# A two-layer decoder trunk: the 14 additions that close Strassen's scheme in each FFN, asked for in three portions

## The chip, the cores and the metric

The kernel runs on one core of one Trainium2 chip. The metric is the time of one execution in device microseconds (us). A profiled execution has a span, from its first to its last instruction, and a time of its own that is a little longer.

## The reference

A sequence of 512 tokens with 1024 features goes through two layers: a retention layer with its FFN, then a dilated-attention layer with its FFN. All is float32. Only the FFNs matter here, and both have this form:

```python
def conv_ffn(h, w_up, conv_w, conv_b, w_down):
    S = h.shape[1]
    u = h @ w_up                                   # 1024 -> 2 * 2816
    gate, val = u[..., :D_FF], u[..., D_FF:]
    gp = jnp.pad(gate, ((0, 0), (CONV_WIDTH - 1, 0), (0, 0)))
    conv = conv_b
    for i in range(CONV_WIDTH):
        conv = conv + conv_w[i] * gp[:, i:i + S]
    return (jax.nn.gelu(conv, approximate=True) * val) @ w_down   # 2816 -> 1024
...
x = x + rmsnorm(f, norm_ffn_post[layer])
```

## The kernel before, in words

**Products in three matmuls.** Every float32 operand is split into a high part (a cast to fp32r) and a low part (what the cast lost). A product is then high x high, high x low and low x high: `mm3`, lines 210 to 212. For a weight unit of 128x1024 this means one load into a `raw` tile (line 157, on SP's queue, three buffers), one cast on ScalarE into `whi` (line 170) and one subtraction on VectorE into `wlo` (line 171); `whi` and `wlo` have five buffers each, so a cast waits until TensorE has finished with the unit five places earlier.

**The FFN.** The 2816 inner features are 22 rows of 128 features, f = 0 to 21. `up(f)` loads two units of w_up (gate and value), forms two products of 24 matmuls each (8 steps of 3) into two PSUM tiles `pm`, and `gated` turns them into an activation (convolution at lines 599 to 604, gelu at 605, product at 607, split at 612). In this document "f=19 gate" is the unit, or the product, of the gate half of row 19.

**Strassen's scheme.** The rows 2 to 17 go through w_down in four groups of four rows. A group (`down7`, `contract7`) forms seven products instead of eight, in the order 1, 7, 6, 4, 5, 2, 3, each for two blocks of rows r = 0, 1: 12 matmuls of the `po` kind per number, 84 per group. Each result is added from PSUM into a running sum in SBUF (line 273). The sums lie in the tiles that are free for that time: product 1 in the first halves of m0 and m1, product 3 in their second halves, product 4 and 5 in the halves of m2 and m3, and products 2, 6 and 7 in tiles called q0, q1 and q2, which take the places of the residual tiles x0, x1 and x2. For that, x was written out to DRAM before (`away`, line 696). PSUM has two buffers for the sums of r = 0 and four, shared with `pm`, for those of r = 1.

**The end of the scheme.** The last group is formed behind `up(18)`. `combine7` (line 327) then joins the seven sums: for each r it adds 6+=1, 1+=2, 5+=6, 3+=5, 5+=7, 4+=6, 4+=7, so 14 additions of 128x512 on VectorE (line 332). Behind it, in the text of the program, x0 to x3 are loaded back (line 710; x3 shared its place with no sum, so its load comes much earlier), then come `up(19)` to `up(21)`, then `contract` over the rows 0 and 1, and then `finish`, which contracts over the rows 18 to 21, normalises, and adds to x (line 351).

**What sets the order.** Each engine runs its instructions in a fixed order, and each queue its transfers. The program is compiled by a scheduler that takes the text's order as priority and a model of the times to decide when an instruction is placed on its engine; in the stretches that matter here it is free on all engines (`finish` fixes the order of VectorE and GpSimd by hand). What an engine waits for at run time is set by data and by buffers.

Of the kernel before, what the change touches and what calls it, by code (L numbers as in the profile page):

```python
# [10 lines left out]
F32 = mybir.dt.float32  # L11
# [6 lines left out]
P = 128  # L18
SEQ = 512
D = 1024  # L20
NB = SEQ // P
# [54 lines left out]
def _run(gen):  # L76
    for _ in gen:
        pass
# [18 lines left out]
def trunk(ctx: ExitStack, tc: tile.TileContext, a, out):  # L97
    nc = tc.nc

    const = ctx.enter_context(tc.tile_pool(name="const", bufs=1))  # L100
# [5 lines left out]
    away = [dram.tile([P, D], F32, name=f"away{b}") for b in range(NB)]  # L106
# [6 lines left out]
    x = [const.tile([P, D], F32, name=f"x{b}", tag=f"x{b}") for b in range(NB)]  # L113
# [94 lines left out]
    def mm3(o, l, r, start, stop):  # L208

        nc.tensor.matmul(o, lhsT=l[0], rhs=r[0], start=start, stop=False)  # L210
        nc.tensor.matmul(o, lhsT=l[0], rhs=r[1], start=False, stop=False)  # L211
        nc.tensor.matmul(o, lhsT=l[1], rhs=r[0], start=False, stop=stop)  # L212
# [56 lines left out]
    def accumulate(src, dst, first):  # L269
        if first:  # L270
            nc.scalar.copy(out=dst, in_=src)
        else:
            nc.vector.tensor_add(out=dst, in0=src, in1=dst)  # L273

    def contract(left, w, first, tag="po", after=None):


        for b in range(NB):
            for c in range(2):
                po = ps.tile([P, 512], F32, name="po", tag=tag, bufs=4 if tag == "mm" else 2)  # L280
                for j in range(len(w)):
                    mm3(po, left(j, b), (w[j][0][:, half(c)], w[j][1][:, half(c)]), j == 0, j == len(w) - 1)
                    if j < len(w) - 1:
                        yield
                accumulate(po, m[b][:, half(c)], first)
                if after is not None:
                    after(b, c)
                yield
# [38 lines left out]
    def combine7(q):  # L327

        for r in range(2):
            q1, q2, q3, q4, q5, q6, q7 = (q[i][r] for i in range(1, 8))  # L330
            for dst, src in ((q6, q1), (q1, q2), (q5, q6), (q3, q5), (q5, q7), (q4, q6), (q4, q7)):
                nc.vector.tensor_add(out=dst, in0=dst, in1=src)  # L332

    E = mybir.EngineType
    F4=1
# [251 lines left out]
    def ffn(l, pool, post, then, late, ahead=()):  # L587
        w_up, w_down = a["ffn_w_up"][l], a["ffn_w_down"][l]
        cw = lambda i, f: cols[l][:, i * FT + f : i * FT + f + 1]
        with pool as tmp:  # L590
# [30 lines left out]
            SEVEN = 2, 18  # L621
# [65 lines left out]
            def down(fs, act, pool=None):  # L687
                w = [unit(w_down[f * P : (f + 1) * P, :], pool=pool if i < 3 else None) for i, f in enumerate(fs)]
                return lambda j, b: [t[:, blk(b)] for t in act[j]], w
# [7 lines left out]
            q = {i: [m[r + 2 * h][:, half(c)] for r in range(2)] for i, h, c in ((1, 0, 0), (3, 0, 1), (4, 1, 0), (5, 1, 1))}  # L697
# [3 lines left out]
            for f in range(2, FT):  # L701
                acts[f] = up(f)
                f0 = f - 4
                if seven(f0) and f0 % 4 == 2:
                    down7(f0, [acts[f0 + i] for i in range(4)], group[f0], f0 == SEVEN[0], q)
                    if f == SEVEN[1]:
                        combine7(q)
                        for b in range(NB):
                            x[b] = const.tile([P, D], F32, name=f"x{b}", tag=f"x{b}")
                            nc.sync.dma_start(out=x[b], in_=away[b])  # L710
                if seven(f) and f % 4 == 1:
                    group[f - 3] = list(sx)
            _run(contract(*down(range(2), [acts[0], acts[1]]), False))
            prev = (range(FT - 4, FT), [acts[f] for f in range(FT - 4, FT)])
            l, w = down(*prev, tmp)
# [415 lines left out]
```

## Time and profile before

| what | value |
|---|---|
| time, median of 3 runs | 1720.17 us (1720.15 to 1720.6) |
| time of the profiled execution | 1719.35 us |
| its span | 1717.5 us |
| mean granted TensorE clock | 0.993 of full speed |
| TensorE busy | 1682.1 us (98%) |
| VectorE busy | 1083.7 us (63%) |
| ScalarE busy | 661.9 us (39%) |
| GpSimd busy | 389.8 us (23%) |

The first FFN lies at about 411 to 798 us of the span, the second from about 1340 us to the end. In a timeline row the first number is the start (us from the span's start), the second the length in us, then engine, line, operation and tiles, and in brackets how long the engine was idle before it and what ended that. PE is TensorE, DVE VectorE, ACT ScalarE, POOL GpSimd, SP the queue of the transfers. The matmuls overlap: their lengths are longer than the distance from one start to the next, and it is the distance that counts. Consecutive instructions of VectorE overlap a little at their ends too. Some matmul records are missing from a trace.

### The profile page before, as it was taken

Reading aid. Unit: us, or ns where it says so; the run is one execution under the profiler, and the core shown is the slowest. Engines: PE = TensorE matmul, PEld = TensorE weight load, DVE = VectorE, ACT = ScalarE, POOL = GpSimd, SP = SyncE. Lnnn points to the kernel's source line nnn. Section 1 sums busy time; section 2 is a strip of 40 time slices with the busy share of each in tenths; the row PEclk is TensorE's granted clock in tenths of the full one; section 3 lists DMA queues with packets and bytes.
Section 4 is the critical chain, followed back from the end, with each engine's and each line's share of the span. In section 5 each row is a group of like instructions: output and inputs, shape, how many; then the busy total and the mean of one; then the engine's idle time right before and its main releaser. Section 6 shows DMA issues by size and latency. Waiting matters only on the chain. (4 is left out here: it accounts for less than half of the span.)

```text
span 1717.5 us, 21852 instructions
## 1 busy us (share of the span) xinstructions
PE 1682.1 (98%) x8494; PEld 1394.2 (81%) x8494; DVE 1083.7 (63%) x1718; ACT 661.9 (39%) x1170; POOL 389.8 (23%) x281
## 2 busy tenths in 40 slices
PE   8999999999999999999899999999999999999998
PEld 6888888887888888788788888888887888888876
DVE  4553545558666787868556556566465866777875
ACT  5232322325454444343143243243254545434431
POOL 1000000004000000036756655665531400000003
PEclk9999999999999999999999999999999999999999
DMA  6422323214523422331322322222221533233041
GB/s 208 129 71 86 88 90 92 75 60 157 163 74 99 135 84 77 123 120 51 96 74 74 87 74 67 82 75 78 83 74 58 186 100 111 74 110 123 25 147 49
DMA packets 208565, 164.52 MB, mean 96 GB/s; under 512 B 5245, under 2 KB 182349, under 8 KB 208462
## 3 DMA queue, kind: packets, MB, share of 16 engines
q1 hardware_dynamic: 208462, 163.12, 30.7%
q8 instruction: 67, 1.10, 0.3%
q14 instruction: 36, 0.29, 0.1%
HBM read 156.81 MB, written 6.29 MB: 95 GB/s over the span
## 5 line engine op out<-in xcount | busy, mean ns | idle before, releaser
L171 DVE TENSOR_TENSOR wlo<-raw,whi 128x1024 fp32r<-128x1024 f32 x299 | 405.1, 1359 | 223.7 <-ACT whi L170 222.3
L212 PE MATMUL pm<-hT_hi,wlo 128*128 128x512 f32 (+1 forms) x1424 | 539.3, 379 | 6.8 <-DVE wlo L171 6.8
L210 PE MATMUL pm<-hT_hi,whi 128*128 128x512 f32 (+1 forms) x1424 | 545.8, 383 | 0.0
L211 PE MATMUL pm<-hT_lo,whi 128*128 128x512 f32 (+1 forms) x1424 | 538.9, 378 | 0.0
L170 ACT CAST whi<-raw 128x1024 fp32r<-128x1024 f32 x299 | 313.0, 1051 | 530.7 <-PE pm L211 255.4
L212 PEld LDWEIGHTS pm<-hT_hi,wlo 128*128 128x128 f32 x1424 | 268.6, 189 | 58.1 <-DVE wlo L171 7.7
L210 PEld LDWEIGHTS pm<-hT_hi,whi 128*128 128x128 f32 x1424 | 269.0, 189 | 51.2 <-issue 3.2
L211 PEld LDWEIGHTS pm<-hT_lo,whi 128*128 128x128 f32 x1424 | 269.0, 189 | 48.1 <-DVE hT_lo L201 0.9
L160 POOL TENSOR_TENSOR raw<-raw,cols 128x1024 f32<-128x1024 f32 x72 | 139.7, 1941 | 448.1 <-DMA raw<-in_att_w_kv 374.1
L210 PE MATMUL pm<-whi,hT_hi 128*128 128x512 f32 (+1 forms) x384 | 141.9, 369 | 0.0
L211 PE MATMUL pm<-wlo,hT_hi 128*128 128x512 f32 (+1 forms) x384 | 136.7, 356 | 0.0
L212 PE MATMUL pm<-whi,hT_lo 128*128 128x512 f32 (+1 forms) x384 | 136.7, 356 | 0.0
L369 POOL TENSOR_TENSOR h<-m,gain 128x512 f32<-128x512 f32 x28 | 42.0, 1498 | 397.9 <-issue 329.1
L273 DVE TENSOR_TENSOR m<-po,m 128x512 f32<-128x512 f32 x112 | 75.3, 685 | 45.3 <-PE po L212 45.0
L217 POOL TENSOR_TENSOR r_gn<-v_gn,nhalf 128x1 f32<-128x1 f32 x16 | 8.8, 550 | 357.4 <-DVE v_gn L526 357.4
L211 PE MATMUL po<-wlo,ah 128*128 128x512 f32 x224 | 87.8, 392 | 0.0
L210 PE MATMUL po<-whi,ah 128*128 128x512 f32 x224 | 87.8, 392 | 0.0
L212 PE MATMUL po<-whi,al 128*128 128x512 f32 x224 | 87.6, 391 | 0.0
L210 PEld LDWEIGHTS pm<-whi,hT_hi 128*128 128x128 f32 x384 | 72.9, 190 | 11.5 <-issue 1.0
L211 PEld LDWEIGHTS pm<-wlo,hT_hi 128*128 128x128 f32 x384 | 73.0, 190 | 11.0 <-DVE wlo L171 0.7
L212 PEld LDWEIGHTS pm<-whi,hT_lo 128*128 128x128 f32 x384 | 72.8, 190 | 10.6 <-DVE hT_lo L201 0.2
L602 DVE SCALAR_TENSOR_TENSOR conv<-pm,cols,conv 128x511 f32<-128x511 f32 x88 | 65.6, 746 | 6.6 <-ACT conv L599 5.4
(160 smaller groups left out, 2209.4 us busy)
## 6 DMA issues: line engine op xcount, KB each, us to landing
raw<-in_ffn_w_up SPq DMA_DIRECT2D x88, 512.0 KB, 3.8
raw<-in_att_w_kv SPq DMA_DIRECT2D x48, 512.0 KB, 3.8
raw<-in_ret_w_in SPq DMA_DIRECT2D x47, 512.0 KB, 3.9
raw<-in_ffn_w_down SPq DMA_DIRECT2D x44, 512.0 KB, 3.4
raw<-in_att_w_q SPq DMA_DIRECT2D x24, 512.0 KB, 3.8
raw<-in_ret_w_out SPq DMA_DIRECT2D x16, 512.0 KB, 3.2
away<-x SPq DMA_DIRECT2D x8, 512.0 KB, 3.8
x<-away SPq DMA_DIRECT2D x8, 512.0 KB, 3.2
```

The costliest lines, as they stand in the source:

```text
L160: nc.gpsimd.tensor_mul(out=dst, in0=dst, in1=gain.unsqueeze(2).broadcast_to(list(src.shape)))
L170: nc.scalar.copy(out=hi, in_=raw)
L171: nc.vector.tensor_sub(out=lo, in0=raw, in1=hi.bitcast(F32))
L210: nc.tensor.matmul(o, lhsT=l[0], rhs=r[0], start=start, stop=False)
L211: nc.tensor.matmul(o, lhsT=l[0], rhs=r[1], start=False, stop=False)
L212: nc.tensor.matmul(o, lhsT=l[1], rhs=r[0], start=False, stop=stop)
L217: behind.append(nc.gpsimd.tensor_tensor(out=r, in0=v, in1=nhalf, op=ALU.pow).ins)
L273: nc.vector.tensor_add(out=dst, in0=src, in1=dst)
L369: eng.tensor_mul(out=mg[b][c], in0=m[b][:, half(c)], in1=gain[:, half(c)])
L602: nc.vector.scalar_tensor_tensor(out=t[:, d:], in0=pg[:, : SEQ - d], scalar=cw(i, f), in1=t[:, d:], op0=ALU.mult, op1=ALU.add)
```

## The change

`combine7` becomes a generator that stops after each addition. It is no longer run to its end behind `up(18)`. Instead five additions are drawn from it behind each of `up(19)`, `up(20)` and `up(21)`: 5, 5 and 4. The loads of x move behind the loop, so behind `up(21)` in the text. The additions, their order among themselves and their operands are the same, and both FFNs have the change.

```diff
@@ combine7
             for dst, src in ((q6, q1), (q1, q2), (q5, q6), (q3, q5), (q5, q7), (q4, q6), (q4, q7)):
                 nc.vector.tensor_add(out=dst, in0=dst, in1=src)
+                yield
@@ ffn, loop over f
                 if seven(f0) and f0 % 4 == 2:
                     down7(f0, [acts[f0 + i] for i in range(4)], group[f0], f0 == SEVEN[0], q)
-                    if f == SEVEN[1]:
-                        combine7(q)
-                        for b in range(NB):
-                            x[b] = const.tile([P, D], F32, name=f"x{b}", tag=f"x{b}")
-                            nc.sync.dma_start(out=x[b], in_=away[b])
                 if seven(f) and f % 4 == 1:
                     group[f - 3] = list(sx)
+                if f > SEVEN[1]:
+
+                    left = combine7(q) if f == SEVEN[1] + 1 else left
+                    for _ in range(5):
+                        next(left, None)
+            for b in range(NB):
+                x[b] = const.tile([P, D], F32, name=f"x{b}", tag=f"x{b}")
+                nc.sync.dma_start(out=x[b], in_=away[b])
             _run(contract(*down(range(2), [acts[0], acts[1]]), False))
```

The scheduler turns this into another order on VectorE, on SP's queue and, for a few instructions, on TensorE and ScalarE. It is the same in both FFNs; the rows below are of the first. The names carry the numbers of the program's buffers: q0, q1, q2 are the sums of the products 2, 6 and 7; `po` is a product's PSUM tile; m0 to m3 hold the sums of 1, 3, 4 and 5. Lines from 333 on have a number that is higher by 1 in the changed kernel, and by more behind the loop (line 710 is 716).

VectorE, from the last two PSUM results of the group to the first weight units of `up(19)`, before (wlo_5538 is f=19 gate, wlo_5544 f=19 value, wlo_5611 f=20 gate):

```order
L273 TENSOR_TENSOR m0_83<-po_5498,m0_83 128x512
L332 TENSOR_TENSOR m1_84<-m1_84,q0_3546 128x512
L332 TENSOR_TENSOR m0_83<-m0_83,m2_85 128x512
L273 TENSOR_TENSOR m1_84<-po_5506,m1_84 128x512
L332 TENSOR_TENSOR m2_85<-m2_85,q2_3548 128x512
L332 TENSOR_TENSOR m1_84<-m1_84,m3_86 128x512
L332 TENSOR_TENSOR m3_86<-m3_86,q2_3548 128x512 x2
L171 TENSOR_TENSOR wlo_5538<-raw_5536,whi_5539 128x1024
L171 TENSOR_TENSOR wlo_5544<-raw_5542,whi_5545 128x1024
L171 TENSOR_TENSOR wlo_5611<-raw_5609,whi_5612 128x1024
```

VectorE in the changed kernel, from the first addition of the scheme's end on (wlo_5516 is f=19 gate, wlo_5522 f=19 value, wlo_5594 f=20 gate):

```order
L332 TENSOR_TENSOR q1_3547<-q1_3547,m0_83 128x512
L273 TENSOR_TENSOR m2_85<-po_5450,m2_85 128x512
L171 TENSOR_TENSOR wlo_5516<-raw_5514,whi_5517 128x1024
L273 TENSOR_TENSOR m3_86<-po_5458,m3_86 128x512
L171 TENSOR_TENSOR wlo_5522<-raw_5520,whi_5523 128x1024
L273 TENSOR_TENSOR m2_85<-po_5466,m2_85 128x512
L273 TENSOR_TENSOR m3_86<-po_5474,m3_86 128x512
L332 TENSOR_TENSOR m2_85<-m2_85,q1_3547 128x512
L273 TENSOR_TENSOR q0_3546<-po_5482,q0_3546 128x512
L171 TENSOR_TENSOR wlo_5594<-raw_5592,whi_5595 128x1024
L273 TENSOR_TENSOR q0_3546<-po_5490,q0_3546 128x512
L332 TENSOR_TENSOR m0_83<-m0_83,q0_3546 128x512
```

Before, all 14 additions stand ahead of the first subtraction of `up(19)`. Now one does, and the first four subtractions stand between the results of the products 4 to 3. Behind these rows follow m0's last result, the subtraction of f=20 value, m1's last result, five additions in a row, the subtraction of f=21 gate, two additions, that of f=21 value, and then the last four additions among the convolution and the activation of f=19; the very last one stands behind the activation's product.

SP's queue before, from the load of f=20 gate on (raw_5868 belongs to the next stage; raw_5615 is f=20 value, raw_5682 and raw_5688 are f=21):

```order
L157 DMA raw_5609<-in_ffn_w_up 128x8x128
L157 DMA raw_5868<-in_att_w_kv 128x4x256
L710 DMA x1_5530<-away1_73 128x1024
L710 DMA x0_5528<-away0_72 128x1024
L710 DMA x2_5532<-away2_74 128x1024
L157 DMA raw_5615<-in_ffn_w_up 128x8x128
L157 DMA raw_5682<-in_ffn_w_up 128x8x128
L157 DMA raw_5688<-in_ffn_w_up 128x8x128
L157 DMA raw_5755<-in_ffn_w_down 128x1024
L157 DMA raw_5761<-in_ffn_w_down 128x1024
```

SP's queue in the changed kernel, from the same load on (raw_5598 is f=20 value, raw_5670 and raw_5676 are f=21):

```order
L157 DMA raw_5592<-in_ffn_w_up 128x8x128
L157 DMA raw_5868<-in_att_w_kv 128x4x256
L157 DMA raw_5598<-in_ffn_w_up 128x8x128
L157 DMA raw_5670<-in_ffn_w_up 128x8x128
L157 DMA raw_5676<-in_ffn_w_up 128x8x128
L157 DMA raw_5755<-in_ffn_w_down 128x1024
L157 DMA raw_5761<-in_ffn_w_down 128x1024
L716 DMA x0_5747<-away0_72 128x1024
L157 DMA raw_5831<-in_ffn_w_down 128x1024
L716 DMA x1_5749<-away1_73 128x1024
L716 DMA x2_5751<-away2_74 128x1024
L157 DMA raw_5837<-in_ffn_w_down 128x1024
```

The three loads of x move from ahead of three units of w_up to among the six units of w_down, ahead of the last four of them.

TensorE before, from the end of the group on (pm_5548 and pm_5549 are the products of f=19, pm_5621 is f=20 gate):

```order
L212 MATMUL po_5506<-whi_5447,sx_5116 128x512
L210 MATMUL pm_5548<-hT_hi_87,whi_5539 128x512
L211 MATMUL pm_5548<-hT_lo_88,whi_5539 128x512
L210 MATMUL pm_5549<-hT_hi_87,whi_5545 128x512
L211 MATMUL pm_5549<-hT_lo_88,whi_5545 128x512
L210 MATMUL pm_5621<-hT_hi_87,whi_5612 128x512
L211 MATMUL pm_5621<-hT_lo_88,whi_5612 128x512
L212 MATMUL pm_5548<-hT_hi_87,wlo_5538 128x512
```

TensorE in the changed kernel, from the same place (pm_5526 is f=19 gate):

```order
L212 MATMUL po_5506<-whi_5447,sx_5116 128x512
L210 MATMUL pm_5526<-hT_hi_87,whi_5517 128x512
L211 MATMUL pm_5526<-hT_lo_88,whi_5517 128x512
L212 MATMUL pm_5526<-hT_hi_87,wlo_5516 128x512
L210 MATMUL pm_5526<-hT_hi_87,whi_5517 128x512
L211 MATMUL pm_5526<-hT_lo_88,whi_5517 128x512
```

Before, six matmuls that need no low part stand ahead of the first that does; now it is the third. The number of matmuls is the same: the two pairs of f=19 value and f=20 gate go back to their places.

## The prediction

> **What bounds the kernel now.** I read the page first, then the list of waits, then the timelines of the engines around the end of Strassen's scheme. TensorE is busy nearly throughout, and its waits are short and few; two of them stand on one line:
>
> ```profile
> PE 1682.1 (98%) x8494; PEld 1394.2 (81%) x8494; DVE 1083.7 (63%) x1718; ACT 661.9 (39%) x1170; POOL 389.8 (23%) x281
> PE pm L212 <- DVE wlo L171: 6.8, 2, 3.4
> ```
>
> So the end is set by TensorE, and a change can gain only where TensorE waits or runs slowly. Both waits lie where the change is. TensorE in the first FFN, from the first matmul of the last group through the first products behind it:
>
> ```profile
> 690.69 0.39 PE L210 MATMUL po<-whi,ah 128*128 128x512 f32 x1
> ...
> 709.73 0.39 PE L210 MATMUL pm<-hT_hi,whi 128*128 128x512 f32 x1
> ...
> 710.86 0.39 PE L211 MATMUL pm<-hT_lo,whi 128*128 128x512 f32 x1
> 714.66 0.70 PE L212 MATMUL pm<-hT_hi,wlo 128*128 128x512 f32 x1 [3.41 <-DVE wlo L171]
> 715.16 0.63 PE L210 MATMUL pm<-hT_hi,whi 128*128 128x512 f32 x1
> ...
> 718.15 0.42 PE L211 MATMUL pm<-hT_lo,whi 128*128 128x512 f32 x1
> ...
> 718.64 0.40 PE L210 MATMUL pm<-hT_hi,whi 128*128 128x512 f32 x1
> ...
> 721.62 0.39 PE L210 MATMUL pm<-hT_hi,whi 128*128 128x512 f32 x1
> ```
>
> The group has 84 matmuls in 709.73 - 690.69 = 19.04 us, so one starts every 0.2267 us. Six more start without a low part; the seventh waits for f=19's first low part until 714.66. Then seven starts take 718.15 - 715.16 = 2.99 us, 0.427 each, and only from 718.64 on is the old step back. VectorE in that time:
>
> ```profile
> 699.76 0.68 DVE L332 TENSOR_TENSOR q<-q,m 128x512 f32<-128x512 f32 x1
> 700.41 0.69 DVE L273 TENSOR_TENSOR m<-po,m 128x512 f32<-128x512 f32 x1
> 701.02 0.68 DVE L332 TENSOR_TENSOR q<-q,m 128x512 f32<-128x512 f32 x1
> 701.62 0.69 DVE L332 TENSOR_TENSOR m<-m,q 128x512 f32<-128x512 f32 x1
> ...
> 712.18 1.28 DVE L332 TENSOR_TENSOR m<-m,q 128x512 f32<-128x512 f32 x2
> 713.39 3.49 DVE L171 TENSOR_TENSOR wlo<-raw,whi 128x1024 fp32r<-128x1024 f32 x3
> ```
>
> An addition or a result takes 0.60 us from start to start, a subtraction 3.49 / 3 = 1.16. VectorE does not pause: 14 additions, 14 x 0.60 = 8.4 us, are mixed among the results, and three subtractions come behind them all. Yet their casts were long done; these are ScalarE's rows for f=19 gate, f=19 value, f=20 gate and f=20 value:
>
> ```profile
> 699.05 1.06 ACT L170 CAST whi<-raw 128x1024 fp32r<-128x1024 f32 x1 [1.67 <-PE po L212]
> 701.77 1.06 ACT L170 CAST whi<-raw 128x1024 fp32r<-128x1024 f32 x1 [1.66 <-PE po L212]
> 704.49 1.06 ACT L170 CAST whi<-raw 128x1024 fp32r<-128x1024 f32 x1 [1.66 <-PE po L212]
> 719.78 1.05 ACT L170 CAST whi<-raw 128x1024 fp32r<-128x1024 f32 x1 [14.24 <-DMA raw<-in_ffn_w_up]
> ```
>
> The first subtraction could have begun at 700.1 and began at 713.39. Nothing but its place in VectorE's order holds it.
>
> **The sum.** From the matmul at 709.73 to the one at 721.62 the order counts 29 places: 11.89 us, where 29 x 0.2267 = 6.57. The loss is 5.32 us: 714.66 - 710.86 - 0.23 = 3.57 of waiting, and 1.75 of slow steps behind it. In the second FFN the same rows stand:
>
> ```profile
> 1638.66 0.39 PE L210 MATMUL pm<-hT_hi,whi 128*128 128x512 f32 x1
> ...
> 1639.80 0.39 PE L211 MATMUL pm<-hT_lo,whi 128*128 128x512 f32 x1
> 1643.59 0.79 PE L212 MATMUL pm<-hT_hi,wlo 128*128 128x512 f32 x1 [3.40 <-DVE wlo L171]
> ...
> 1646.69 0.40 PE L210 MATMUL pm<-hT_hi,whi 128*128 128x512 f32 x1
> ...
> 1650.33 0.39 PE L210 MATMUL pm<-hT_hi,whi 128*128 128x512 f32 x1
> ```
>
> Again 29 places, 11.67 us: a loss of 5.10, of which 1643.59 - 1639.80 - 0.23 = 3.56 is waiting and 1.54 slow steps. If both go, the gain is 10.42 us.
>
> The slow steps are the granted clock. The program has a shorter wait too, where a layer begins, and three stretches show the clock behind the wait at 714.66, behind a wait that the first rival is about, and behind the shorter one:
>
> ```profile
> 1340.14 0.66 PE L266 MATMUL pt<-ident,h 128*128 128x128 f32 x4 [2.25 <-DVE h L258]
> ...
> 715.20:718.00 2.80, 2.80 (x8) 2.21 (x7) 1.68 (x2) 0.00 (x0) 0.00 (x0) 0.50 0.87 279
> 776.20:779.20 3.00, 3.00 (x11) 2.56 (x10) 2.88 (x3) 2.12 (x5) 1.83 (x2) 0.50 0.00 0
> 1342.00:1346.00 4.00, 4.00 (x19) 3.28 (x19) 3.90 (x6) 2.38 (x8) 2.44 (x4) 1.00 0.33 131
> ```
>
> The column behind the five engines is the clock: 0.50 behind the wait of 3.41 us, 1.00 behind that of 2.25. In the long stretches without a wait, such as the 84 steps of 0.2267, no slow step shows; so I count the 1.75 + 1.54 in full. The waits alone are 3.57 + 3.56 = 7.13 us, which is the lower end of the gain if the clock falls elsewhere instead. [...]
>
> **What the changed order makes late, on VectorE.** I walk its new rows with 0.60 and 1.16. One addition (699.76) and a result (700.41), then f=19 gate's subtraction, 701.0 to 702.2. A result to 702.8; f=19 value's cast ends at 701.77 + 1.06 = 702.83, its subtraction at 704.0. Two results and an addition to 705.8; product 2's first result, which TensorE ends at about 705.7, to 706.5; f=20 gate to 707.7. A result, an addition, a result, to 709.5; f=20 value to 710.7. A result and five additions to 714.3; f=21 gate to 715.5; two additions; f=21 value to about 717.9, its cast waiting until TensorE is through with f=19 gate at 709.73 + 24 x 0.2267 = 715.2. Every unit is needed at its product's third matmul: f=19 gate at 710.2, and then one more every 5.44 us: 715.6, 721.1, 726.5, 731.9, 737.4. So the six have 8.0, 11.6, 13.4, 15.8, 16.4 and 19.5 us to spare. The last addition stands behind the product of f=19's activation, which needs f=19 value at 720.6: it ends at about 722.
>
> What lies under the moved additions: nine of them, 5.4 us, now run after 711, beside the products of f=19 and f=20. They cost nothing while the subtractions keep those margins, and they can gain nothing either, since TensorE waits for no addition there. They put f=19's activation back by up to four additions, 2.4 us; its reader is the contraction behind the 144 matmuls of `up(19)` to `up(21)`, at 709.73 + 144 x 0.2267 = 742.4, 20 us later.
>
> The subtractions now stand ahead of results, and TensorE needs the PSUM tiles back. The tightest: product 3 for r = 0, begun at 690.69 + 72 x 0.2267 = 707.0, uses the tile that product 5's result leaves at 704.6. That is 2.4 us to spare, so 0; each us beyond would cost one.
>
> **On SP's queue.** Its transfers from the loads of x on, before:
>
> ```profile
> 707.17 6.65 SPq L710 DMA_DIRECT2D x<-away  x3
> 714.63 3.13 SPq L157 DMA_DIRECT2D raw<-in_ffn_w_up  x3
> 722.12 12.40 SPq L157 DMA_DIRECT2D raw<-in_ffn_w_down  x6
> ```
>
> Next its wait for the additions (us in all, times, longest), from its list of waits, and how long the weight loads of 700 to 740 took to land:
>
> ```profile
> SPq L710 <- DVE m L332: 19.4, 3, 13.8
> ...
> DMA to landing us min/median/max: 4.4/4.9/6.4
> ```
>
> The loads of x waited for additions, 13.8 us at the longest, and held f=20 value and f=21 back to 714.63. Now those three follow their buffers: each waits for the subtraction three units earlier, so 702.2, 704.0 and 707.7. The first two units of w_down follow at 710.7 and 715.5, x0 once product 2's last addition is through (716), a third unit at 718, x1 and x2 at 721 to 722, and the last three units from about 724 to 729, against a last one at 734.5 before. They are first used together with f=18 to 21, 48 matmuls behind 742.4, at 753.3. With 6.4 to land and 1.06 + 1.16 for cast and subtraction, a unit may be asked for as late as 744: 15 us to spare. The row that reads x0 first:
>
> ```profile
> 769.21 2.43 DVE L351 SCALAR_TENSOR_TENSOR x<-h,r_rms,x 128x512 f32<-128x512 f32 x2 [0.45 <-POOL r_rms L217]
> ```
>
> stands 45 us behind x2's request, and a load needs 6.4 at most. So SP's part is 0; beyond 15 us of delay each us would cost one.
>
> **The rivals.**
>
> *First, the wait at the end of the FFN becomes cheaper too.* Once TensorE is 5.3 us ahead, the next wait falls elsewhere against whatever grants the clock. That wait and the same step at full speed:
>
> ```profile
> 772.30 0.49 PE L210 MATMUL po<-whi,ah 128*128 128x512 f32 x1
> 775.75 1.56 PE L266 MATMUL pt<-ident,h 128*128 128x128 f32 x8 [2.96 <-DVE h L256]
> ...
> 779.66 0.40 PE L211 MATMUL po<-wlo,ah 128*128 128x512 f32 x1
> ...
> 783.56 1.04 PE L266 MATMUL pt<-ident,h 128*128 128x128 f32 x8
> 784.36 0.47 PE L210 MATMUL po<-whi,ah 128*128 128x512 f32 x1
> ```
>
> From 775.75 to 779.66 are eight transposes and six steps, 3.91 us; at full speed 784.36 - 783.56 + 6 x 0.2267 = 2.16. That is 1.75 us. Full speed returns at about 718.2, 779.6 and, in the second FFN, 1646.6: 61.4 and 928.4 us apart, which is 18 and 272 times 3.41. If the clock is judged in fixed windows of 3.41 us, one ends at 769.4, and the wait, moved to 767.5 to 770.4, is split by it into 1.9 and 1.0 us, like the 2.25 that kept the clock at 1.00. The gain is then 10.42 + 1.75 = 12.2 us, 1708.0. Against it: nothing in the trace fixes such a window to the program, and if one falls wholly on the wait of 2.25 us instead, the same price comes on top and the gain is 8.7 us, 1711.5. [...]
>
> *Second, the change doesn't do what it says:* the wait moves on to a later unit with the same length, because VectorE has the same work and a later subtraction is now behind the additions (f=21 gate, behind five). For it speaks that VectorE is nearly full from 699.8 to 711 in the walk above. Against it stand the margins of 8 to 19 us. The time would be 1720.2.
>
> *Third, slower: TensorE waits for PSUM.* VectorE takes its rows in order, so a subtraction that waits for a cast or a load holds all results behind it, and TensorE with them. The place is product 3, r = 0. It begins to cost when VectorE is 2.4 us later than in the walk, and beats the gain when it is 2.4 + 5.2 = 7.6 us later in each FFN; at 10 us late the time is 1720.2 + 2 x 2.4 = 1725. Against it: the casts ahead ended at 700.1, 702.8 and 705.6 in the trace, each before its turn or within 0.1 us of it.
>
> **How the numbers follow.** The profiled execution took 1719.35 us, 1.85 more than its span, and that rest stays. 1719.35 - 10.42 = 1708.93. The median of the runs is 0.82 us above it: 1720.17 - 10.42 = 1709.75, my forecast, 1709.8, with a chance of 0.62. The first rival has 0.27. A part of the gain (one FFN alone, 5 us) has 0.05, the second rival 0.04, the third 0.02. The range goes from 1707.2 (the first rival, 0.8 lower for the spread of the runs) to 1713.0 (only the waits go, 7.13 us). A measurement can tell 0.2%, 3.4 us, from no change. So faster has 0.62 + 0.27 + 0.05 = 0.94, the same 0.04, slower 0.02.
>
> **What would show it.** Right: no wait of TensorE on line 171, 29 places behind the group in 6.6 us, clock 1.00 there, f=19 gate's low part near 702, the last addition near 722, the contraction about 32.7 us behind the group's end (38.0 before). Wrong: a wait on line 212 or 210 for a subtraction or a PSUM result inside `up(19)` to `up(21)`, a wait for units of w_down in the contraction, or a clock of 0.50 at a place where it was 1.00.

## The result, and the profile after

| | before | after |
|---|---|---|
| median | 1720.38 us (1720.15 to 1722.35, 4 runs) | 1708.97 us (1706.58 to 1712.33, 4 runs) |
| ratio, 95% interval | 1 | 0.9933 (0.9921 to 0.9945) |
| profiled execution, its span | 1719.35 us, 1717.5 us | 1706.58 us, 1704.7 us |

The kernel is faster by 0.67%, 11.4 us between the medians; the prediction was 1709.8 us. A second timing of the changed kernel, six runs, gave 1709.07 us and 0.993 (0.9915 to 0.9946).

The top of TensorE's list of waits, after (engine, line, tile waited for: us in all, times, longest):

```profile
PE pt L266 <- DVE h L258: 8.6, 8, 2.0
```

The entry of 6.8 us on line 212 is gone. What is left at the top are the waits at the layers' norms, which led the list before too, with 8.8 us. TensorE in the first FFN, from the end of Strassen's last group to the first matmul of the contraction:

```profile
709.75 0.39 PE L210 MATMUL pm<-hT_hi,whi 128*128 128x512 f32 x1
...
710.20 0.39 PE L212 MATMUL pm<-hT_hi,wlo 128*128 128x512 f32 x1
...
716.55 0.39 PE L210 MATMUL pm<-hT_hi,whi 128*128 128x512 f32 x1
...
742.39 0.39 PE L210 MATMUL po<-whi,ah 128*128 128x512 f32 x1
```

The third matmul now takes the low part at once. Places 0 and 30 of the order are 709.75 and 716.55: 6.80 us, 0.2267 each, no slow step among them. The contraction follows the group's end by 742.39 - 709.75 = 32.64 us, which is 144 x 0.2267; before it was 747.69 - 709.73 = 37.96. VectorE's new rows (the six subtractions, and the last addition):

```profile
701.04 1.22 DVE L171 TENSOR_TENSOR wlo<-raw,whi 128x1024 fp32r<-128x1024 f32 x1
...
702.88 1.22 DVE L171 TENSOR_TENSOR wlo<-raw,whi 128x1024 fp32r<-128x1024 f32 x1
...
706.48 1.22 DVE L171 TENSOR_TENSOR wlo<-raw,whi 128x1024 fp32r<-128x1024 f32 x1
...
709.41 1.22 DVE L171 TENSOR_TENSOR wlo<-raw,whi 128x1024 fp32r<-128x1024 f32 x1
...
714.15 1.22 DVE L171 TENSOR_TENSOR wlo<-raw,whi 128x1024 fp32r<-128x1024 f32 x1
...
716.49 1.22 DVE L171 TENSOR_TENSOR wlo<-raw,whi 128x1024 fp32r<-128x1024 f32 x1
...
721.86 0.69 DVE L332 TENSOR_TENSOR m<-m,q 128x512 f32<-128x512 f32 x1
```

f=19 gate's low part is there at 702.3; TensorE asks for it at 710.2. SP's queue, after (in the last row the next stage's first weights):

```profile
702.28 5.81 SPq L157 DMA_DIRECT2D raw<-in_ffn_w_up  x3
710.66 5.08 SPq L157 DMA_DIRECT2D raw<-in_ffn_w_down  x2
716.00 0.33 SPq L716 DMA_DIRECT2D x<-away  x1
...
723.70 5.01 SPq L157 DMA_DIRECT2D raw<-in_ffn_w_down  x3
731.23 0.38 SPq L157 DMA_DIRECT2D raw<-in_att_w_kv  x1
```

In the second FFN the contraction follows the group's end by 32.64 us as well (37.74 before).

### The profile page after: what moved, and what is told of

The parts are those of the page before. It is cut to its first block, busy times and chain, and to the rows that moved or that the text cites. A ratio compares the mean times of both kernels' runs of the same rounds, so it can differ in the third digit from the quotient of the medians.

```text
span 1704.7 us, 21864 instructions
## 1 busy us (share of the span) xinstructions
PE 1676.2 (98%) x8494; PEld 1390.3 (82%) x8494; DVE 1081.4 (63%) x1718; ACT 662.4 (39%) x1170; POOL 393.7 (23%) x281
## 5 line engine op out<-in xcount | busy, mean ns | idle before, releaser
L210 PEld LDWEIGHTS pm<-whi,hT_hi 128*128 128x128 f32 x384 | 72.8, 190 | 11.4 <-issue 1.0
```

## The experiments

The question was which part of the change does it. **Theory A** (the prediction's): the place of f=19 gate's subtraction in VectorE's order, ahead of the additions instead of behind them. **B:** the loads of x, which no longer hold SP's queue for additions, so that the units of w_up arrive earlier. **C:** the spreading itself, in portions; additions in one piece would only move the wait to a later unit. Besides, the clock's part and the slack of the neighbours were to be measured. "Stretch" below is the time from the end of Strassen's last group to the contraction, in the first and the second FFN of the profiled execution. Where a gain is given in us, it is the difference to the median of the kernel before on the same chip: 1720.77 us for the first four runs of the table below the changed kernel's, 1720.94 for the next three and 1720.71 for the last two.

| run | median (range, runs) | ratio (95%) | stretch |
|---|---|---|---|
| before | 1720.38 (1720.15 to 1722.35, 4) | 1 | 37.96, 37.74 |
| after | 1708.97 (1706.58 to 1712.33, 4) | 0.9933 (0.9921 to 0.9945) | 32.64, 32.64 |
| loads_moved_only | 1721.98 (1720.53 to 1724.65, 10) | 1.0003 (0.9994 to 1.0013) | 38.90, 37.94 |
| one_unit_ahead | 1713.55 (1712.21 to 1714.09, 4) | 0.9958 (0.9943 to 0.9973) | 32.64, 32.64 |
| ten_ahead | 1714.41 (1712.07 to 1718.17, 5) | 0.9965 (0.9952 to 0.9978) | 34.54, 34.55 |
| one_portion | 1710.71 (1707.43 to 1711.46, 4) | 0.9944 (0.9928 to 0.9961) | 32.64, 32.64 |
| first_ffn_only | 1714.64 (1711.66 to 1717.52, 10) | 0.9964 (0.9953 to 0.9976) | 32.64, 37.67 |
| additions_on_gpsimd | 1714.68 (1713.08 to 1717.98, 9) | 0.9964 (0.9953 to 0.9975) | 32.64, 32.64 |
| again | 1709.07 (1707.55 to 1712.32, 6) | 0.993 (0.9915 to 0.9946) | 32.64, 32.63 |
| one_unit_loads_last | 1711.91 (1710.74 to 1716.38, 4) | 0.9953 (0.9938 to 0.9968) | 32.64, 32.64 |
| gpsimd_loads_last | 1711.47 (1709.83 to 1711.91, 4) | 0.9943 (0.9927 to 0.996) | 32.64, 32.64 |

### Only the loads of x move

The additions stay behind `up(18)`; the loads of x go behind the loop, and are tied behind the last load of `up(21)` (`loads` collects the loads of line 157).

```diff
...
                     if f == SEVEN[1]:
                         combine7(q)
-                        for b in range(NB):
-                            x[b] = const.tile([P, D], F32, name=f"x{b}", tag=f"x{b}")
-                            nc.sync.dma_start(out=x[b], in_=away[b])
...
+            for b in range(NB):
+                x[b] = const.tile([P, D], F32, name=f"x{b}", tag=f"x{b}")
+                with tc.issue_after(loads[-1]):
+                    nc.sync.dma_start(out=x[b], in_=away[b])
```

> Half of the change alone: the 14 additions stay where they were before, behind up(18), and only the loads of x move, on SP's queue behind the last unit of f=21. Theory A (the place of f=19 gate's subtraction in VectorE's order sets the time): that subtraction still stands behind all 14 additions, so TensorE waits 3.4 us for it in each FFN again, the 29 places behind the group take 11.9 and 11.7 us, and the time is that of before, 1720 us, although f=20 value and f=21 are now asked for near 714 or earlier. Theory B (the loads of x held the weight loads of f=20 and f=21 back, and that was the loss): the gain is here, 1709 to 1711 us.

Measured: 1.0003, no change. TensorE's list of waits holds the old entry:

```profile
PE pm L212 <- DVE wlo L171: 6.8, 2, 3.4
```

and VectorE subtracts as late as before, three units behind the last addition:

```profile
712.00 1.29 DVE L332 TENSOR_TENSOR m<-m,q 128x512 f32<-128x512 f32 x2
713.20 3.50 DVE L171 TENSOR_TENSOR wlo<-raw,whi 128x1024 fp32r<-128x1024 f32 x3
```

SP's queue asks for f=20 value and f=21 no earlier than before (714.63, with the group's end 0.18 later there as well):

```profile
714.45 2.64 SPq L157 DMA_DIRECT2D raw<-in_ffn_w_up  x3
```

The loads of x no longer stand ahead of these three, and yet they wait: for the `raw` buffers, the first of which is freed by f=19 gate's subtraction, which ends at 714.42. So moving the loads of x alone brings neither an earlier load nor time. Earlier loads had nothing to win either: TensorE waited for none of these units, here or before. In both profiles its only wait between the group's end and the contraction is the one on line 212. B falls.

The first stretch, 38.90 us, is 0.94 longer than before, with the same wait of 3.41 us. The clock (the number behind the five engines, as in the prediction) stays at 0.50 for 6.83 us behind that wait; in the profile before it was half as long, 3.41 us (714.79 to 718.20):

```profile
713.04:719.87 6.83, 5.39 (x13) 4.24 (x14) 3.73 (x5) 1.04 (x1) 0.00 (x0) 0.50 0.59 166
```

### Only one unit goes ahead

All 14 additions and the loads of x stay behind `up(18)`; only f=19 gate is asked for ahead of them.

```diff
...
                     if f == SEVEN[1]:
+                        gate = cols_unit(w_up, (f + 1) * P)
                         combine7(q)
```

> The other half in its smallest form: the additions and the loads of x stay behind up(18) in the text, and only the first unit of up(19) (f=19 gate: load, cast, subtraction) is asked for ahead of them. 13 additions still stand ahead of f=19 value's subtraction, and the additions are not spread over three rows. Theory A: f=19 gate is done near 702, f=19 value near 715 (needed at 715.6), so no wait of TensorE on line 171, 29 places in 6.6 us in both FFNs, 1709 us give or take 2 for the clock elsewhere. Theory B: 1720 us. Theory C (what counts is that VectorE's work is spread over up(19) to up(21)): no gain or a small part of it, since 13 of 14 additions are still in one stretch.

Measured: 0.9958, a gain of 7.2 us, and both stretches are 32.64. One subtraction's place in each FFN is enough to take both waits on line 212 away. That is A. It speaks against B as well: the units of f=21 are asked for at 716.70 and 718.44 here, no earlier than before, and the stretches are short all the same. What is missing to the changed kernel's gain, some 4 us, lies elsewhere; TensorE in the contraction has a wait that neither kernel shows:

```profile
748.36 0.50 PE L210 MATMUL po<-whi,ah 128*128 128x512 f32 x1 [1.48 <-DVE m L273]
```

It is followed back further below, with the two runs made for it. What is missing besides its 1.48 us was not followed.

### Ten additions ahead

From the changed kernel: ten additions are drawn behind `up(18)`, four behind `up(19)`, and f=19 gate's subtraction is tied behind the tenth. The scheduler put it behind the eleventh.

```diff
...
-            def up(f):
-                w = cols_unit(w_up, f * P), cols_unit(w_up, FF + f * P)
+            def up(f, last=None):
+                if last is None:
+                    w = (cols_unit(w_up, f * P),)
+                else:
+                    raw = fetch(cols_of(w_up, f * P))
+                    with tc.issue_after(last):
+                        w = (parts(raw),)
+                w += (cols_unit(w_up, FF + f * P),)
...
-                acts[f] = up(f)
+                acts[f] = up(f, added if f == SEVEN[1] + 1 else None)
...
-                    for _ in range(5):
-                        next(left, None)
+                    for _ in range((10, 4, 0, 0)[f - SEVEN[1]]):
+                        added = next(left, None)
```

> The changed kernel with a shorter wait put back: ten additions are asked for behind up(18), four behind up(19), and f=19 gate's subtraction is tied behind the tenth addition. By VectorE's rows it then stands behind 11 additions, three fewer than before, so it ends 3 x 0.60 = 1.8 us earlier, near 712.7, and TensorE waits about 1.8 us in each FFN instead of 3.57. If the halved clock needs a wait of some 3 us (theory A's second term): clock 1.00 behind it, 29 places in 6.6 + 1.8 = 8.4 us, and about 3.6 us in all on the changed kernel, 1712 to 1713 us. If every wait brings the slow steps with it: 29 places in about 10 us, 1716 us.

Measured: 0.9965, a gain of 6.4 us. The stretches are 1.90 and 1.91 us longer than in the changed kernel; 10.42 - 3.81 = 6.6. The wait in the first FFN, and the steps behind it:

```profile
712.92 0.50 PE L212 MATMUL pm<-hT_hi,wlo 128*128 128x512 f32 x1 [1.60 <-DVE wlo L171]
713.26 0.39 PE L210 MATMUL pm<-hT_hi,whi 128*128 128x512 f32 x1
713.49 0.40 PE L211 MATMUL pm<-hT_lo,whi 128*128 128x512 f32 x1
```

The wait is back, shorter by three additions (3.41 - 1.60 = 1.81 = 3 x 0.60): it follows the place in the order addition by addition. Behind it the steps are 0.23 us, not 0.427. So a wait of 3.4 us cost 5.3 and 5.1, and one of 1.6 us cost 1.9: the slow steps belong to the long wait. Nor was the short wait spared by where it lay against the moments at which the clock falls and returns, which within one execution lie whole multiples of 3.4133 us apart (from the profiles, further below). In this execution the clock first falls to 0.50 behind another wait, at 771.80:

```profile
771.80:778.62 6.82, 5.70 (x18) 4.83 (x19) 5.70 (x7) 3.03 (x8) 4.58 (x6) 0.50 0.00 0
```

Steps of 3.4133 us counted from there lie at 710.36 and 713.77, and the wait, 711.32 to 712.92, lies whole between them. In the second FFN (1636.11 to 1637.71, between 1635.37 and 1638.79) it is the same.

### All 14 in one piece, behind `up(19)`

```diff
...
-                    for _ in range(5):
+                    for _ in range((0, 14, 0, 0)[f - SEVEN[1]]):
                         next(left, None)
```

> The three portions become one: all 14 additions are asked for behind up(19), the loads of x stay behind the loop. f=20 gate's subtraction then stands behind all 14 additions and is done near 716.0, needed at 721.1. Theory A: as the changed kernel, no wait on line 171, 29 places in 6.6 us, 1709 us give or take 2. Theory C: slower than the changed kernel by a part of its gain, with a wait inside f=20.

Measured: 0.9944 (0.9928 to 0.9961), which overlaps with the changed kernel's interval; both stretches 32.64. VectorE, the first subtraction and the densest row of additions:

```profile
701.07 1.22 DVE L171 TENSOR_TENSOR wlo<-raw,whi 128x1024 fp32r<-128x1024 f32 x1
...
711.47 2.49 DVE L332 TENSOR_TENSOR m<-m,q 128x512 f32<-128x512 f32 x4
```

C falls: the three portions are not needed, only that the first units of `up(19)` come first.

### The change in the first FFN alone

```diff
...
-                    for _ in range(5):
+                    for _ in range(((0, 5, 5, 4), (14, 0, 0, 0))[l][f - SEVEN[1]]):
                         next(left, None)
```

and the loads of x directly behind the additions in the second.

> The change in the first FFN alone; the second has the old order. Theory A: the terms add: 32.64 us from the group's end to the contraction in the first FFN, 37.7 in the second, and about 5 us less than before in all, 1715 us give or take 2. Rival: the gain of the first FFN is given back by a wait behind it (at the FFN's end or in the attention's start), 1720 us.

Measured: 0.9964, a gain of 6.3 us; the interval, 4.1 to 8.1 us, holds the 5.32 of the first FFN. In its profile the old wait stands in the second FFN alone:

```profile
1636.32 0.80 PE L212 MATMUL pm<-hT_hi,wlo 128*128 128x512 f32 x1 [3.40 <-DVE wlo L171]
```

The two FFNs' terms add.

### The additions on GpSimd

The kernel before, with nothing moved but the engine.

```diff
-                nc.vector.tensor_add(out=dst, in0=dst, in1=src)
+                nc.gpsimd.tensor_add(out=dst, in0=dst, in1=src)
```

> The kernel before, with the 14 additions at their old place in the text but on GpSimd instead of VectorE: VectorE's order has no addition ahead of the subtractions, and its work in the stretch is 8.4 us less. Theory A: f=19 gate's subtraction is done near 702, no wait on line 171, the stretch from the group's end to the contraction 32.64 us in both FFNs, 1709 us give or take 2, as in the changed kernel, although GpSimd needs about 14 x 1.5 = 21 us for the additions and x1, x0 and x2 are loaded only near 722 to 727, among f=21 and w_down. If the loads of x or the late sums do harm, the wait shows in f=21 value or the contraction, up to 5 us in each FFN.

Measured: 0.9964, a gain of 6.3 us. With the additions off VectorE the subtractions are early and both stretches are 32.64, so A holds from another side: the additions need not be late, they must not stand ahead. But the wait in the contraction is there again, longer:

```profile
748.63 0.77 PE L210 MATMUL po<-whi,ah 128*128 128x512 f32 x1 [3.47 <-DVE m L273]
```

Behind it the clock is at 0.50 from 748.69 to 752.11. The wait and half of that time are 3.47 + 1.71 = 5.2 us, an estimate of what this cost; the changed kernel's gain on the same chip is 11.9 us, 5.6 more than here.

### What the wait in the contraction hangs on

In one_unit_ahead and additions_on_gpsimd the same chain leads to it. GpSimd scales the next stage's weights (line 160) when they land; ScalarE casts them (line 170), and f=21's convolution stands behind that cast in its order. In one_unit_ahead, SP, GpSimd and ScalarE:

```profile
735.66 0.38 SPq L157 DMA_DIRECT2D raw<-in_att_w_kv  x1
```

```profile
741.03 3.90 POOL L160 TENSOR_TENSOR raw<-raw,cols 128x1024 f32<-128x1024 f32 x2 [306.43 <-DMA raw<-in_att_w_kv]
```

```profile
742.96 1.05 ACT L170 CAST whi<-raw 128x1024 fp32r<-128x1024 f32 x1 [3.88 <-POOL raw L160]
743.92 0.77 ACT L599 ACTIVATE conv<-pm,cols 128x512 f32<-128x512 f32 x1
```

ScalarE idles 3.88 us for the weights, and the convolution, whose own data has long been there, waits with it. VectorE then makes f=21's activation late, and with it the result that frees TensorE's tile. In the changed kernel the same rows of GpSimd and ScalarE, and VectorE's product of f=21's activation:

```profile
735.34 1.90 POOL L160 TENSOR_TENSOR raw<-raw,cols 128x1024 f32<-128x1024 f32 x1 [302.37 <-DMA raw<-in_att_w_kv]
```

```profile
737.27 1.05 ACT L170 CAST whi<-raw 128x1024 fp32r<-128x1024 f32 x1 [3.02 <-POOL raw L160]
738.23 0.77 ACT L600 ACTIVATE conv<-pm,cols 128x512 f32<-128x512 f32 x1
```

```profile
742.66 0.69 DVE L608 TENSOR_TENSOR act<-conv,pm 128x512 f32<-128x512 f32 x1 [2.09 <-PE pm L212]
```

Here the activation waits for TensorE, 2.09 us, and not the other way round. Counted from the group's end (709.75 there, 711.36 in one_unit_ahead) the convolution starts at 28.48 here and at 32.56 there: 4.08 us later, more than the slack of 2.09.

Two things could hold SP back in those two runs: the loads of x, which wait for additions there, or f=19 value's subtraction, which in one_unit_ahead still stands behind the additions and frees a `raw` buffer late. So both runs were repeated with the loads of x tied behind the last load of w_down:

```diff
+            for b in range(NB):
+                x[b] = const.tile([P, D], F32, name=f"x{b}", tag=f"x{b}")
+                with tc.issue_after(loads[-1]):
+                    nc.sync.dma_start(out=x[b], in_=away[b])
             return finish(l, w, post, then, ahead, early=tmp)
```

> As one_unit_ahead (f=19 gate ahead of the additions, the additions behind up(18)), but the loads of x, x3 among them, stand on SP's queue behind the last unit of w_down. It asks which of two things delayed the next stage's weight load to 735.66 there, and with it GpSimd's scaling, ScalarE's cast at 742.96, the convolution of f=21 behind that cast, and the PSUM result behind the convolution, for which TensorE waited 1.48 us near 748. If the loads of x did (11.1 us of waiting on the queue): no such wait now, the next stage's load near 731, 1709 to 1711 us. If the late subtraction of f=19 value did (its load buffer goes to f=21 gate, which was asked for only at 716.70): the same wait of about 1.5 us, 1711 to 1713 us. In both, 32.64 us from the group's end to the contraction.

> As additions_on_gpsimd, but the loads of x stand behind the last unit of w_down. There the additions took GpSimd until 723, x1, x0 and x2 were loaded at 714.4, 716.9 and 723.2 ahead of f=21 value and of w_down, and TensorE waited 3.47 us near 748 for a PSUM result behind f=21's convolution, which stood behind ScalarE's cast of a unit of the next stage. If the loads of x on the queue are the cause: that wait is gone, the next stage's load near 730, and the time is that of the changed kernel, 1709 us give or take 2. If it is GpSimd, late with its scaling because of the additions: the wait stays, 1713 to 1715 us.

Measured: 0.9953 and 0.9943; both intervals overlap with those of the runs they repeat. In one_unit_loads_last TensorE waits 1.65 us:

```profile
748.22 0.50 PE L210 MATMUL po<-whi,ah 128*128 128x512 f32 x1 [1.65 <-DVE m L273]
```

and in gpsimd_loads_last 0.43 us:

```profile
748.26 0.50 PE L210 MATMUL po<-whi,ah 128*128 128x512 f32 x1 [0.43 <-DVE m L273]
```

The line is the same, but the way to it is another. In one_unit_loads_last, ScalarE and then VectorE:

```profile
737.09 0.78 ACT L599 ACTIVATE conv<-pm,cols 128x512 f32<-128x512 f32 x1
...
745.19 1.05 ACT L170 CAST whi<-raw 128x1024 fp32r<-128x1024 f32 x1 [4.80 <-POOL raw L160]
746.15 0.61 ACT L200 CAST ah<-act 128x512 fp32r<-128x512 f32 x1
```

```profile
746.79 0.77 DVE L201 TENSOR_TENSOR al<-act,ah 128x512 fp32r<-128x512 f32 x1 [2.21 <-ACT ah L200]
```

The convolution of f=21 now stands ahead of the cast and starts 27.40 us behind the group's end, in time; in gpsimd_loads_last too (738.35 - 710.95). What stands behind the cast is the high part of f=21's activation (line 200). VectorE waits 2.21 us for it (0.93 in gpsimd_loads_last) with the low part (line 201), and the next results from PSUM stand behind that. So moving the loads of x also changed ScalarE's order, and the waits of these two runs can't be compared with those that they were to explain. Of the two expectations, the size of the wait and the time of one_unit_loads_last fit the second theory, but not by its way; gpsimd_loads_last, 1711.47 us with a wait of 0.43, fits neither.

What the two runs do show is the request of the next stage's weights. Counted from the group's end, it moved from 26.00 to 21.26 us with the additions on GpSimd, where the changed kernel has 21.48: there it was the loads of x that held SP. With one unit ahead it moved only from 24.30 to 23.82: there it was mostly not the loads, which leaves the buffers that the late subtraction frees. That part was not tried by itself. But the weights landed little sooner for it, or later. SP and GpSimd in one_unit_loads_last:

```profile
731.28 2.13 SPq L717 DMA_DIRECT2D x<-away  x4
733.51 0.45 SPq L157 DMA_DIRECT2D raw<-in_att_w_kv  x1
```

```profile
743.26 7.91 POOL L160 TENSOR_TENSOR raw<-raw,cols 128x1024 f32<-128x1024 f32 x4 [310.35 <-DMA raw<-in_att_w_q]
```

From the request to GpSimd's start are 9.75 us (9.24 in gpsimd_loads_last: 732.21 to 741.45), against 4.11 in the changed kernel, 5.37 in one_unit_ahead and 5.67 in additions_on_gpsimd. In all five, GpSimd starts 0.38 or 0.39 us after the last part of the w_kv load has landed (742.88 here; the row names the w_q load, parts of which landed at the same time). What differs is that four loads of x, 2 MB, had been sent right ahead. That these slowed the landing is the likely reason, not a shown one. So in all four runs the late weights hold ScalarE, in the first two ahead of f=21's convolution and in the last two ahead of the split of its activation; none of them is a better kernel than the changed one.

### The changed kernel once more

> The changed kernel once more, for its spread and its ratio. Its four times so far lie at 1706.6 to 1712.3 us with mean clocks of 0.998 to 0.993, those of before closer together. Theory A: the stretch from the group's end to the contraction is 32.64 us in both FFNs again, whatever the time; what differs between executions lies elsewhere, where the clock falls to 0.50 behind other waits (those near 411, 770 and 840 us). Rival: the additions' waits come and go, so this stretch itself differs between executions. Median 1708 to 1711 us.

> The changed kernel, one more profile for the clock. Theory: within one execution the returns to full speed lie a whole number of 3.41 us apart, as 718.2, 779.6 and 1646.6 did before, but the grid lies elsewhere against the program in each execution, so that each time other waits are followed by a clock of 0.50. Rival: the grid stands still against the start of the program, and the same waits are hit as in the first profile of the changed kernel, none but the one near 844 us.

Measured: 1709.07 us (1707.55 to 1712.32) and, in the single execution, 1711.94 us. Three profiled executions of the same program now have spans of 1704.7, 1710.5 and 1710.1 us, with the same stretches. What differs is the clock behind the waits at the norms and at the attention's start. TensorE at the first FFN's start, where each execution waits 2.03 us, and behind the wait at that FFN's end; after, in stretches (us, busy time of five engines, granted clock, DMA):

```profile
411.50:415.50 4.00, 4.00 (x23) 3.38 (x22) 4.00 (x6) 3.01 (x8) 2.43 (x2) 1.00 0.04 11
770.50:773.50 3.00, 3.00 (x18) 2.62 (x19) 2.88 (x4) 1.72 (x5) 2.19 (x3) 1.00 0.00 0
```

and again:

```profile
411.50:415.50 4.00, 3.34 (x13) 2.87 (x13) 4.00 (x5) 2.25 (x6) 3.17 (x4) 0.61 0.31 93
772.00:777.00 5.00, 4.15 (x17) 3.45 (x18) 4.88 (x7) 2.80 (x7) 2.98 (x4) 0.72 0.00 0
```

The same wait of 2.03 us left the clock at 1.00 in one execution and at 0.61 in the other (0.50 from 412.34 to 415.76). By the group's end the second is 712.14 - 709.75 = 2.39 us behind the first, of which 0.93 were there before that wait ended (412.16 against 411.23). At the end it is 5.8 us behind, with more such places in between. This is what spreads the changed kernel's runs, as far as it was followed.

A clock of 0.50 at a place where it was 1.00 was one of the prediction's signs of being wrong. It came here, at the start of both FFNs (412.34 and 1337.35). But the first profile of the same program does not have it, so it belongs to the execution and not to the change.

## Why the prediction was right

**The two terms.** Predicted were 5.32 and 5.10 us from the removed wait and its slow steps. The stretches became shorter by 37.96 - 32.64 = 5.32 and 37.74 - 32.64 = 5.10. Right to the last digit, because both losses were read as differences of starts in one order of matmuls, as many matmuls lie between afterwards, and the comparison is with the same profile that they were read from. The waits of 3.57 and 3.56 are firm. The slow steps are not: in loads_moved_only the same wait in the first FFN cost 38.90 - 32.64 = 6.26 us, so 2.69 of slow steps and not 1.75, and in first_ffn_only the second FFN's cost 37.67 - 32.64 = 5.03, so some 1.5. How near 10.42 comes to the gain between any other two executions is in part luck. That the slow steps go with the wait was an argument then; ten_ahead shows it: behind 1.6 us of waiting there are none.

**The cause.** "Nothing but its place in VectorE's order holds it": shown by one_unit_ahead (that one place moved, both waits gone), by ten_ahead (three additions fewer ahead of it, a wait shorter by three additions) and, from the other side, by additions_on_gpsimd (no additions ahead of it, both waits gone) and loads_moved_only (the loads moved, that place not, nothing gained).

**VectorE's walk.** The six subtractions were predicted to start at 701.0, 702.8, 706.5, 709.5, 714.3 and 716.7; measured are the rows above, none off by more than 0.25 us. The last addition was to end at 722 and ends at 722.55. No unit and no PSUM tile was late: the second and the third rival did not come about.

**SP's queue.** The requests came as walked (w_up by 702.28 + 5.81 = 708.1, x0 at 716.00, the last w_down by 723.70 + 5.01 = 728.7), and the part is 0 as predicted. One reading was wrong: the loads of x did not hold f=20 value and f=21 back to 714.63, since without them ahead these are asked for at 714.45 (loads_moved_only); the buffers did, behind the same late subtractions. And "15 us to spare" was the margin of w_down's units only. The tightest reader of that queue was not walked: the next stage's weights, which by way of GpSimd and ScalarE's order hold f=21's convolution. Their margin is 2.09 us, and the kernel before had 1.54; in one_unit_ahead and additions_on_gpsimd it was overdrawn and cost 1.48 and 3.47 us. The change did not meet it, since it sends these weights earlier: at 731.23, against 735.99 before. For this reader the predicted 0 came out right without a reason given, which is luck.

**The first rival.** It said that the wait at the end of the FFN would keep full clock too, and that this is worth 1.75 us. In the profiled execution after, it did keep it (1.00 from 770.50 on, above). But the gain was 0.43 us, not 1.75: the term was mis-sized, because the working stopped at the last slow step. TensorE's rows after, from that wait to the next:

```profile
770.45 1.09 PE L266 MATMUL pt<-ident,h 128*128 128x128 f32 x8 [2.96 <-DVE h L256]
777.66 1.06 PE L266 MATMUL pt<-ident,h 128*128 128x128 f32 x8 [0.87 <-DVE h L256]
...
792.80 0.63 PE L266 MATMUL pt<-ident,h 128*128 128x128 f32 x4 [0.89 <-DVE h L256]
```

At full speed TensorE reaches the transposes at 777.66 before their data and waits 0.87 us there, which it did not before. From 770.45 to 792.80 are 22.35 us; before, from 775.75 to 798.53, 22.78. And it is no property of the changed kernel: in the run again the same wait has 0.72 behind it. It is a draw of each execution, as the doubt in the prediction had it, and the 0.27 belonged into the spread around one forecast instead of into a second one.

**The size of the whole.** The profiled execution lost 12.8 us of span, where the sum was 10.42. From the traces: 5.30 up to the first contraction, 0.43 at the end of that FFN, 1.21 where the attention begins (798.53 to 849.36 before, 792.80 to 842.42 after), 0.46 in the rest up to the second FFN's group, 5.10 there; 0.3 are left. The 1.21 are not the change's: in the two other executions of the changed kernel that part takes 49.40 and 51.33 us. The medians differ by 11.4 and 11.9 us, 1.0 and 1.5 above the sum; with single executions 5.8 us apart that is within what the clock's draw can give, and what is left of it was not followed.

**The clock's grid.** The first rival supposed windows of 3.41 us. The length is in the profile before: the four stretches with a clock of 0.50 that lie ahead of 1700 us (714.79 to 718.20, 776.23 to 779.64, 847.91 to 854.73, 1643.21 to 1646.63) last 3.41, 3.41, 6.83 and 3.41 us. Within an execution the moments at which full speed returns behind the waits, from 411 us on, lie whole multiples of 3.4133 us apart: before 718.20, 779.64, 854.73 and 1646.63, which is 0, 18.0, 40.0 and 272.0; in loads_moved_only 719.87, 781.31, 856.40 and 1648.30, which is 0, 18.0, 40.0 and 272.0; in again 415.76, 777.57, 852.66 and 1340.77, which is 0, 106.0, 128.0 and 271.0. From one execution to the next this grid lies elsewhere against the program (415.76 there, 414.92 in again_one_look). All twelve profiles have the wait of 2.03 us near 411, and the clock behind it went with the grid: in four of them (again, again_one_look, one_unit_ahead, gpsimd_loads_last) the wait lies whole between two neighbouring points of it, and the clock is at 0.50 behind it; in the other eight a point splits it, into parts of at most 1.94 us, and the clock stays at 1.00. In again it lies from 410.13 to 412.16, between 408.93 and 412.34; before, from 409.20 to 411.23, with a point at 411.00. What sets the grid no run shows. A wait of some 3 us, of which the expectation of ten_ahead spoke, was more than the clock needed to fall: 2.03 us of waiting, whole between two points, were enough in four executions. And the slow steps have no fixed price: behind the two waits of 3.4 us every profile that has one shows slow steps, but they cost from 1.5 us (first_ffn_only) to 2.7 us (loads_moved_only), so the 3.29 us counted here are one draw.

## What to carry to other kernels

When an engine that has slack delays the one that bounds, look at what stands ahead of the awaited instruction in its order, not at how much it has to do: one subtraction in each FFN, moved ahead of the additions, made the two stretches 10.4 us shorter together, and VectorE's work stayed the same. Before moving work behind others, walk every queue to its tightest reader, which may belong to the next stage: here 2.09 us of slack lay there, not the 15 that the own stage's loads had. And price a slow stretch up to the next wait, not to its last slow step, since the wait may swallow the difference: here 1.75 us of slow steps at the FFN's end were worth 0.43.

## What the runs showed of the hardware

Two things were not expected. Behind a wait of 2.03 us at the same place of the same program the clock was at 0.50 for 3.42 us in one execution (again) and at 1.00 in another (after), with the grid of 3.4133 us lying elsewhere; one of 1.60 us, whole between two points of the grid, left no slow steps in either FFN (ten_ahead, stretches longer by 1.90 and 1.91 us in all).

And with the additions on GpSimd, those took 1.28 to 2.38 us each (20 of one form: least, median and largest in ns), where VectorE needs 0.60 from start to start:

```profile
L332 POOL TENSOR_TENSOR m<-m,q x20: 1279/1730/2375, 702.7 to 1650.1; 128x512 f32<-128x512 f32 x20
```

VectorE's own subtraction takes 1.22 us in the changed kernel's six rows. In the same stretch the two engines' rows interlock:

```profile
702.74 1.28 POOL L332 TENSOR_TENSOR m<-m,q 128x512 f32<-128x512 f32 x1
702.77 2.34 DVE L171 TENSOR_TENSOR wlo<-raw,whi 128x1024 fp32r<-128x1024 f32 x1
704.10 2.17 POOL L332 TENSOR_TENSOR m<-m,q 128x512 f32<-128x512 f32 x1
```

The subtraction that starts 0.03 us behind an addition takes 1.12 us longer than usual; the next addition, which starts 1.01 us before that subtraction ends, takes 0.89 longer than the shortest. The rows up to 724 go on like this: an addition that starts during a subtraction, or with it, takes 2.17 to 2.38 us, and any other 1.28 to 1.30. VectorE's additions from PSUM (line 273) show no such lengthening: 0.67 or 0.68 us each beside GpSimd's additions. So in these rows, of a subtraction and an addition, the one that started later took longer by about what was left of the other. Both read two tiles in SBUF, line 273 one; whether that is the reason no run shows.
